# A hybrid decoder block on one Trainium2 core: where the pieces of the MLP's weight sums are made

## The chip, the core and the metric

The kernel runs on one core of a Trainium2 chip. Five engines work side by side, each with its own queue of instructions: TensorE (PE, matmuls), VectorE (DVE), ScalarE (ACT), GpSimd (POOL) and SyncE (SP). In this kernel SP issues most of the DMAs, and POOL and ACT the others. The metric is the time of one execution in device microseconds; less is better.

## What is computed

The block works on S = 2048 tokens of D = 1024 channels in float32. Cut to what matters:

```python
def reference(x, norm_pre_mix, w_in, ..., w_mlp_in, w_mlp_out, norm_post_mlp):
    h = _rmsnorm(x, norm_pre_mix)
    proj = einsum('bsd,de->bse', h, w_in)            # q, k, v, u, z, two gates
    y_attn = _mixer_dilated_attention(q, k, v)       # windows 128, 512, 2048 at dilations 1, 4, 16
    y_gmlp = _mixer_chunked_gmlp(u, z, ...)          # chunks of 128 tokens
    merged = gate_a * (y_attn @ w_branch_attn) + gate_b * (y_gmlp @ w_branch_gmlp)
    x = x + _rmsnorm(merged @ w_out, norm_post_mix)
    h = _rmsnorm(x, norm_pre_mlp)
    a = relu(h @ w_mlp_in)                           # 1024 -> 4096
    y = (a * a) @ w_mlp_out                          # 4096 -> 1024
    return x + _rmsnorm(y, norm_post_mlp)
```

## The kernel before

**Products.** Every float32 operand is split into a high and a low part, and a product is three matmuls (high x high, low x high, high x low). The two large products of the MLP go further: they are cut into quadrants, twice over, and each level needs seven products of sums and differences of quadrants instead of eight. So the first MLP product, w_mlp_in, has an outer level of seven **phases** (o = 0 to 6) and in each phase eight **stages** (two 128-column tiles of the hidden layer each; stages are counted through, so stage 8 is the first of phase o = 1). A stage is seven **products** of six matmuls (L1549). The text counts products through from 0, 56 to a phase, and calls the phases first to seventh.

**What a stage needs.** Its weights come by `load_ha` as the tile `hraw` and are made into half-sums `hs` by `combine` (L1387 to L1402, on POOL, ACT and DVE in turn). The load of a stage takes the buffer of the stage two before it, so it waits until that one's last half-sum, L1402, is done. The activations' quadrants come as `hb` and are split into `spot` tiles. Products land in PSUM tiles `ha`, `hb`, `hc`; DVE (L1563, L1565) and ACT (L1561) add them into the outputs `X`. In the second, fourth and fifth phase a quadrant is first gathered in a stage tile `e` (L1563 makes it, L1565 adds to it). These e tiles live in a pool `rx` under two tags, "xs" and "c1", four buffers each.

**Outer sums.** In the first phase eight `outer_load` / `outer_sum` / `outer_store` steps build sums of the activations' quadrants: three loads `ot`, one sum on DVE (L1504), one on POOL (L1506), one store to `tqd` (L1509). Their tiles use the same two tags of `rx`. The second phase reads `tqd` back as `hb`.

**Pieces of weight sums.** In the third to the sixth phase the weights are no quadrants of w_mlp_in but sums S1 to S4 of them. They are the same for all tokens, and are made ahead in 16 pieces (t = 0 to 15), each four sums of a 128 x 512 tile, stored in DRAM (`wsd`), and loaded from there by `load_ha`. There are two ways to make one:
- In part 2 of the kernel (`merge` and `out_block` for the four chunks of 512 tokens, in the order 2, 3, 0, 1). A generator `w_piece` runs in two calls of `next_piece`: the first issues two loads of 512 KB (`trw`, `tqw`) on SP; the second does four sums on DVE (L1311, L1312, L1314, L1315) and two stores of 512 KB from POOL's queue (L1313, L1316). `trw` and `tqw` have one buffer each. `W_EARLY` pieces are made so, with two `t_piece` of the same kind for the activations between them. `PIECE_AT` says at which of the eight tiles of each chunk's merge a call stands; every out block of the first three chunks has one more, and of the last chunk only the first.
- In the MLP. `w_load` (four loads of 256 KB to `wt`, L1518), four `w_sum` (DVE L1523, POOL L1525, DVE L1527, POOL L1529) and `w_store` (four stores of 256 KB, L1535), all DMAs on SP. Their tiles again use the tags "c1" and "xs" of `rx`, by turns. A table `todo` says after which product each step is written.

**Out block.** For each 128 tokens it multiplies by w_out, adds the result into x (`xr`, L1261), normalizes to `y1` (L1266), transposes y1 on PE (`pt`, L1271), and stores it. The last chunk's out blocks (1,0) to (1,3) lie beside the opening of the MLP.

**What sets the order.** PE's order is written out by hand. The other engines run what the program issues for them in the order of its schedule, and in the MLP as it is written. Each waits at its first instruction that isn't ready; so does SP with its DMAs.

```python
for n in range(8):
    t = 4 + 5 * n
    for f, d, args in ((outer_load, 0, ()), (outer_sum, 4, (0,)), (outer_sum, 6, (2,)), (outer_store, 9, ())):
        later(t + d, f, n, *args)
```

Of the kernel before, what the change touches and what calls it, by code (L numbers as in the profile page):

```python
# [20 lines left out]
KT = 8  # L21
# [21 lines left out]
def block_kernel(ctx, tc, a, out):  # L43
# [1110 lines left out]
    def load_y(c, engs=(("act", "dve"),)):  # L1154
        cs = slice(c * 512, (c + 1) * 512)
        yt = [bot.tile([P, 2, 512], F32R, name=f"yt{c}{k}", tag=f"yt{k}") for k in range(6)]
        for k in range(6):
            split_in(yt[k], ya_d[k, :, cs] if k < 2 else yg_d[k - 2, :, cs], None, *engs[k % len(engs)])
        return yt
# [143 lines left out]
    def w_piece(t):  # L1303

        w, v = (ttp.tile([P, 2, 512], F32, name=f"{n}w{t}", tag=n, bufs=1) for n in ("tq", "tr"))
        for z, n in ((v, t + NF // 2), (w, t)):
            sp.dma_start(z.rearrange("p a c -> p (a c)"), a["w_mlp_in"][n].rearrange("p k c -> p (k c)"))
        yield
        a11, a12, a21, a22 = w[:, 0], w[:, 1], v[:, 0], v[:, 1]
        q, f = divmod(t, 2)  # L1310
        dve.tensor_add(a22, a21, a22)  # L1311
        dve.tensor_sub(a21, a11, a21)  # L1312
        pool.dma_start(ws_d[q][:, 2:4, f], v)  # L1313
        dve.tensor_sub(a11, a22, a11)  # L1314
        dve.tensor_sub(a12, a12, a11)  # L1315
        pool.dma_start(ws_d[q][:, 0:2, f], w)  # L1316
        yield

    W_EARLY = 13
    pieces = deque([w_piece(t) for t in range(W_EARLY - 2)] + [t_piece(0), t_piece(1)] +  # L1320
                   [w_piece(t) for t in range(W_EARLY - 2, W_EARLY)])
    piece = []
    PIECE_AT = {2: (5, 7), 3: (1, 3, 5, 7), 0: (1, 3, 5, 7), 1: (0, 1, 2, 3, 4, 6, 7)}

    def next_piece():
        with behind():
            if piece:
                next(piece.pop(), None)
            elif pieces:
                piece.append(pieces.popleft())  # L1330
                next(piece[0])

    def merge_pieces(c, dt):
        if dt in PIECE_AT[c]:
            next_piece()
# [11 lines left out]
    NQ, HQ = NF // 2, NF // 4  # L1347
# [166 lines left out]
    def w_load(t):  # L1514

        outer_t["w", t] = [rx.tile([P, 512], F32, name=f"wt{t}{m}", tag="xs" if (t - W_EARLY) % 2 else "c1", bufs=4) for m in range(4)]
        for m, z in enumerate(outer_t["w", t]):
# [131 lines left out]
    for n, c in enumerate(chunks):  # L1649
        if n:  # L1650
            mg = merge(c, yt, {0: flush, 2: flush}, lambda dt: merge_pieces(c, dt))
        for i in range(4):
            b = out_block(c, i, mg, flush_older)
            next(b)
            last.append(b)
            if n < 3 or not i:
                next_piece()
            if n < 3 and not i:
                yt = load_y(chunks[n + 1])
                for dt, wch in ((0, 0), (0, 1), (1, 0), (1, 1), (2, 0), (2, 1), (3, 0), (4, 0)):  # L1660
                    with behind():
                        load_gate(chunks[n + 1], dt, wch)
            if n == 3 and i == 1:
                e2r.close()
                egx.close()
                rx = stack(e3, "rx", 1, side="right")
                r4 = stack(e3, "r4", 1, side="right")
                for m in range(4):
                    w = r4.tile([P, 2, 512], F32R, name=f"spot{m}", tag=f"spot{m}")
                    spots.append((w[:, 0], w[:, 1]))  # L1670
                for m in range(2):
                    w = [gtp.tile([P, 512], F32R, name=f"spot{4 + m}{h}", tag=f"gt{m}", bufs=3 - m) for h in range(2)]
                    spots.append(w)
                fifth = gtp.tile([P, 2, 256], F32, name="fifth", tag="gt0", bufs=3)
                first_op(0)
                load_ha(0)
                first_op(1)
                load_ha(1)
                first_op(2)
                for g in sum_ha(0):  # L1680
                    pass
                for j in range(2):
                    for kk in range(2):
                        first_split(j, kk)
                for g in sum_ha(1):
                    pass
                for kk in range(2):
                    first_split(2, kk)
# [225 lines left out]
                       (7, first_split, (6, 0)), (8, first_split, (6, 1)), (9, flush, ())):  # L1914
        later(k, f, *args)
    for n in range(8):
        t = 4 + 5 * n
        for f, d, args in ((outer_load, 0, ()), (outer_sum, 4, (0,)), (outer_sum, 6, (2,)), (outer_store, 9, ())):
            later(t + d, f, n, *args)
    for n in range(NF // 2 - W_EARLY):  # L1920
        t = 7 * 2 * HQ + 6 + 6 * n
        for f, d, args in ((w_load, 0, ()), (w_sum, 4, (0,)), (w_sum, 5, (1,)), (w_sum, 6, (2,)), (w_sum, 7, (3,)),
                           (w_store, 9, ())):
            later(t + d, f, W_EARLY + n, *args)
    for q in range(HQ):
        t = 7 * (5 * HQ + 4) + 19 * q // 2
# [131 lines left out]
```

## Time and profile before

| | |
|---|---|
| time, median of 3 runs | 2632.99 us (2631.65 to 2633.84) |
| the profiled execution | 2633.62 us |
| its span, first to last instruction | 2631.9 us |
| mean granted clock of PE | 0.992 |
| busy: ACT, POOL | 1095.0 us (42%), 1364.3 us (52%) |
| part 2's last out blocks and the first phase | to 1490.5 us |
| second, third, fourth phase | 1490.5 to 1567.5, to 1657.3, to 1734.5 us |

The time of the profiled execution is longer than its span by what lies around it. The rows of the trace below have, in a timeline: start, duration, engine, line, operation, the tiles written and read, the shape, and in brackets the idle time of the engine just before with what ended it. In a list of waits: who waited, for whom, the total in us, how often, the longest. In a group of one tile's instructions: least, median and longest duration in ns, and the first and last start in us. A window's row ends with PE's granted clock, the DMA engines' busy share and GB/s.

### The profile page before, as it was taken

The numbers are of one execution on the slowest core, as the hardware profiler recorded it, in microseconds if no ns is written. First come the engines' busy times: TensorE is split into PE (matmuls) and PEld (weight loads), VectorE is DVE, ScalarE is ACT, GpSimd is POOL, SyncE is SP. The second block draws the span as 40 slices with busy tenths as digits, with TensorE's granted clock in tenths as the row PEclk, the third lists the DMA queues.
The fourth block names the chain that finished last, engine by engine and source line by source line (L and its number), as shares of the span: only waits on it lengthen the run. The fifth ranks groups of instructions, "written<-read, shape, count | busy, mean of one in ns | idle before, by whom it ended". The sixth has DMA issues, their size and how long they took to land. (4 is left out here: it accounts for less than half of the span.)

```text
span 2631.9 us, 35699 instructions
## 1 busy us (share of the span) xinstructions
PE 2561.3 (97%) x12122; PEld 2127.4 (81%) x12122; DVE 1854.8 (70%) x3187; ACT 1095.0 (42%) x2316; POOL 1364.3 (52%) x1265
## 2 busy tenths in 40 slices
PE   9999999999999999999998998999999999999998
PEld 8888888888888887788776886877777888888886
DVE  5676675434433456866667999899898888788867
ACT  5213111254455444544435532433225555555555
POOL 0363354365455554311114656767798677677634
PEclk9999999999999999999999999999999999999999
DMA  8779778888898889776777466456875221222235
GB/s 322 285 245 327 257 234 283 299 276 264 284 303 234 234 293 350 260 246 241 251 236 278 164 179 216 138 183 184 255 248 168 89 88 50 87 94 83 89 119 209
DMA packets 412136, 568.69 MB, mean 216 GB/s; under 512 B 58801, under 2 KB 247473, under 8 KB 410930
## 3 DMA queue, kind: packets, MB, share of 16 engines
q1 hardware_dynamic: 385872, 502.63, 58.4%
q0 software_dynamic: 16192, 57.16, 5.6%
q10 hardware_dynamic: 9890, 6.62, 0.8%
q8 instruction: 96, 1.57, 0.2%
q14 instruction: 86, 0.70, 0.1%
HBM read 362.16 MB, written 204.14 MB: 215 GB/s over the span
## 5 line engine op out<-in xcount | busy, mean ns | idle before, releaser
L1549 PE MATMUL ha<-spot,hs 128*128 128x512 f32 x1344 | 336.3, 397 | 31.1 <-DVE X_yt L1565 9.5
L1549 PEld LDWEIGHTS ha<-spot,hs 128*128 128x128 f32 x1344 | 253.4, 190 | 95.5 <-DVE e L1563 9.9
L1857 PE MATMUL ya<-spot,s 128*128 128x512 f32 x1344 | 323.6, 389 | 2.4 <-DVE X_yt L1865 2.4
L1857 PEld LDWEIGHTS ya<-spot,s 128*128 128x128 f32 x1344 | 252.1, 188 | 55.5 <-issue 1.8
L1549 PE MATMUL hc<-spot,hs 128*128 128x512 f32 x672 | 174.0, 395 | 3.1 <-DVE e L1565 1.7
L728 PE MATMUL g<-opA,spots 128*128 128x512 f32 x672 | 171.4, 399 | 2.1 <-DVE cv L760 2.1
L1857 PE MATMUL yc<-spot,s 128*128 128x512 f32 x672 | 170.5, 389 | 0.0
L728 PE MATMUL g<-opB,spots 128*128 128x512 f32 x648 | 164.0, 397 | 0.0
L1549 PEld LDWEIGHTS hc<-spot,hs 128*128 128x128 f32 x672 | 127.6, 191 | 33.4 <-DVE e L1565 3.4
L96 PE MATMUL x<-hT_a,wq 128*128 128x512 f32 x384 | 149.7, 390 | 0.0
L97 PE MATMUL x<-hT_a,wq 128*128 128x512 f32 x384 | 149.4, 389 | 0.0
L98 PE MATMUL x<-hT_a,wq 128*128 128x512 f32 x384 | 149.4, 389 | 0.0
L1857 PEld LDWEIGHTS yc<-spot,s 128*128 128x128 f32 x672 | 126.1, 188 | 26.2
L728 PEld LDWEIGHTS g<-opA,spots 128*128 128x128 f32 x672 | 121.6, 189 | 24.3 <-issue 2.5
L79 POOL TENSOR_TENSOR spots<-gr,spots 128x512 fp32r<-128x512 f32 x98 | 128.7, 1317 | 21.8 <-DMA gr<-in_w_in_dram 7.7
L79 POOL TENSOR_TENSOR spot<-w2r,spot 128x512 fp32r<-128x512 f32 x79 | 112.1, 1442 | 45.3 <-ACT spot L71 45.3
L1721 ACT ACTIVATE sraw<-sraw 128x1024 f32<-128x1024 f32 x128 | 134.7, 1052 | 2.0 <-DMA sraw<-sd 0.3
L728 PEld LDWEIGHTS g<-opB,spots 128*128 128x128 f32 x648 | 116.9, 188 | 21.2
L71 ACT ACTIVATE hl<-r 128x512 fp32r<-128x512 f32 x48 | 30.4, 633 | 236.5 <-POOL r L329 89.0
L978 DVE TENSOR_REDUCE o<-po 128x256 f32<-128x512 f32 x48 | 33.2, 692 | 134.0 <-PE po L977 134.0
L73 POOL TENSOR_SCALAR spots<-gr 128x512 fp32r<-128x512 f32 x86 | 54.4, 633 | 131.5 <-PE g L728 93.8
L73 POOL TENSOR_SCALAR wq<-wq_r 128x1024 fp32r<-128x1024 f32 x24 | 32.6, 1362 | 136.8 <-PE va L98 87.5
(460 smaller groups left out, 6851.6 us busy)
## 6 DMA issues: line engine op xcount, KB each, us to landing
sraw<-sd SPq DMA_DIRECT2D x128, 256.0 KB, 3.3
qk<-hl SPq DMA_DIRECT2D x24, 1024.0 KB, 5.6
qq<-qk SPq DMA_DIRECT2D x96, 256.0 KB, 5.1
sd<-e SPq DMA_DIRECT2D x64, 256.0 KB, 4.9
hraw<-wsd SPq DMA_DIRECT2D x32, 512.0 KB, 4.6
w2r<-in_w_mlp_out_dram SPq DMA_DIRECT2D x16, 1024.0 KB, 8.7
g<-gated SPq DMA_DIRECT2D x56, 256.0 KB, 5.1
gr<-sgd SPq DMA_DIRECT2D x53, 256.0 KB, 5.0
```

The costliest lines, as they stand in the source:

```text
L71: act.activation(hi, src, AF.Copy)
L73: pool.tensor_scalar(hi, src, 1.0, 1.0, op0=OP.mult, op1=OP.mult)
L79: (pool if lo_eng == "pool" else dve).tensor_sub(lo, src, f32(hi))
L96: pe.matmul(ps, lh, rh, start=start, stop=False)
L97: pe.matmul(ps, lh, rl, start=False, stop=False)
L98: pe.matmul(ps, ll, rh, start=False, stop=stop)
L728: pe.matmul(p, w[:, l, k], h[:, r, k], start=i in (1, 6, 5, 4) and not k and not m, stop=k == 3 and m == 2, skip_group_check=True)
L978: dve.tensor_reduce(ot[:, :, j * 64:(j + 1) * 64], po.rearrange("p (b h e) -> p b e h", b=4, h=2), axis=AX.X, op=OP.add)
L1549: pe.matmul(p, w[:, l, S_AT[i], kk * P:(kk + 1) * P], b[r], start=i in (1, 2, 5) and not kk and not z, stop=kk == 1 and z == 2, skip_group ...
L1721: act.activation(sraw_[n], sraw_[n], func)
L1857: pe.matmul(p, s[:, l], w[r], start=i in (1, 2, 5) and not m and not o, stop=m == 1 and o == 2, skip_group_check=True)
```

## The change

```diff
--- before.py
+++ after.py
@@ -1316,11 +1316,11 @@
         pool.dma_start(ws_d[q][:, 0:2, f], w)
         yield
 
-    W_EARLY = 13
+    W_EARLY = 14
     pieces = deque([w_piece(t) for t in range(W_EARLY - 2)] + [t_piece(0), t_piece(1)] +
                    [w_piece(t) for t in range(W_EARLY - 2, W_EARLY)])
     piece = []
-    PIECE_AT = {2: (5, 7), 3: (1, 3, 5, 7), 0: (1, 3, 5, 7), 1: (0, 1, 2, 3, 4, 6, 7)}
+    PIECE_AT = {2: (3, 5, 7), 3: (0, 2, 4, 6, 7), 0: (1, 3, 5, 7), 1: range(KT)}
 
     def next_piece():
         with behind():
@@ -1653,7 +1653,7 @@
             b = out_block(c, i, mg, flush_older)
             next(b)
             last.append(b)
-            if n < 3 or not i:
+            if n < 3:
                 next_piece()
             if n < 3 and not i:
                 yt = load_y(chunks[n + 1])
@@ -1914,11 +1914,11 @@
                        (7, first_split, (6, 0)), (8, first_split, (6, 1)), (9, flush, ())):
         later(k, f, *args)
     for n in range(8):
-        t = 4 + 5 * n
+        t = 4 + 4 * n
         for f, d, args in ((outer_load, 0, ()), (outer_sum, 4, (0,)), (outer_sum, 6, (2,)), (outer_store, 9, ())):
             later(t + d, f, n, *args)
     for n in range(NF // 2 - W_EARLY):
-        t = 7 * 2 * HQ + 6 + 6 * n
+        t = 38 + 5 * n
         for f, d, args in ((w_load, 0, ()), (w_sum, 4, (0,)), (w_sum, 5, (1,)), (w_sum, 6, (2,)), (w_sum, 7, (3,)),
                            (w_store, 9, ())):
             later(t + d, f, W_EARLY + n, *args)
```

W_EARLY rises from 13 to 14, so 14 pieces are made in part 2 and two in the MLP instead of three. The places of `next_piece` change: merge(2) has tiles 3, 5, 7 instead of 5, 7; merge(3) has 0, 2, 4, 6, 7 instead of 1, 3, 5, 7; merge(1) has all eight instead of seven; out block (1,0) has none any more. That is 32 places for 16 pieces (with the two t_pieces) instead of 30 for 15. The eight outer sums begin at products 4, 8, 12 ... 32 instead of 4, 9, 14 ... 39. The two pieces of the MLP begin at products 38 and 43, in the first phase; the three of before began at 118, 124 and 130, in the third. PE's order is the same.

**The last piece in part 2, on DVE.** Before, behind L1261 of out block (1,0) (which makes xr_10) and the first of its small norm steps. y1_11 is the next out block's tile, r_pm, v_pm and t_pm the norm of y1_10, o_11 a PSUM tile:

```order
L1257 TENSOR_TENSOR y1_11_12726<-o_110_12675,gpost_10420 128x512
L106 RECIPROCAL r_pm10_12656<-r_pm10_12656 128x1
L109 SCALAR_TENSOR_TENSOR t_pm10_12661<-r_pm10_12656,v_pm10_12658 128x1
L113 TENSOR_SCALAR t_pm10_12661<-t_pm10_12661 128x1
L114 TENSOR_TENSOR r_pm10_12656<-r_pm10_12656,t_pm10_12661 128x1
L1266 SCALAR_TENSOR_TENSOR y1_10_12634<-xr_10_12580,r_pm10_12656,gmlp_10421 128x1024
L1311 TENSOR_TENSOR trw12_12577<-trw12_12577 128x512
L1312 TENSOR_TENSOR trw12_12577<-tqw12_12576,trw12_12577 128x512
L1314 TENSOR_TENSOR tqw12_12576<-trw12_12577,tqw12_12576 128x512
L1257 TENSOR_TENSOR y1_11_12726<-o_111_12676,gpost_10420 128x512
L1315 TENSOR_TENSOR tqw12_12576<-tqw12_12576 128x512
```

Now, from that L1261 on:

```order
L1261 SCALAR_TENSOR_TENSOR xr_10_12596<-y1_10_12650,r_post10_12659,xr_10_12596 128x1024
L1311 TENSOR_TENSOR trw13_12562<-trw13_12562 128x512
L105 TENSOR_SCALAR v_pm10_12674<-s2_10_12669 128x1
L1312 TENSOR_TENSOR trw13_12562<-tqw13_12561,trw13_12562 128x512
L1257 TENSOR_TENSOR y1_11_12736<-o_110_12685,gpost_10424 128x512
L1314 TENSOR_TENSOR tqw13_12561<-trw13_12562,tqw13_12561 128x512
L106 RECIPROCAL r_pm10_12672<-r_pm10_12672 128x1
L1315 TENSOR_TENSOR tqw13_12561<-tqw13_12561 128x512
L109 SCALAR_TENSOR_TENSOR t_pm10_12677<-r_pm10_12672,v_pm10_12674 128x1
L113 TENSOR_SCALAR t_pm10_12677<-t_pm10_12677 128x1
L114 TENSOR_TENSOR r_pm10_12672<-r_pm10_12672,t_pm10_12677 128x1
L1266 SCALAR_TENSOR_TENSOR y1_10_12650<-xr_10_12596,r_pm10_12672,gmlp_10425 128x1024
```

The four sums, of piece 13 now instead of 12, stood behind L1266, which makes y1_10, and stand ahead of it.

**The border of the first and second phase, on SP.** Before, from the store of outer sum 6 (ot62) on; hraw_9 and hraw_10 are the weights of stages 9 and 10, hb_20 the activations of the second phase's operand:

```order
L1509 DMA tqd_82<-ot62_13517 128x512
L1378 DMA hraw_9_13621<-in_w_mlp_in_dram 128x2x512
L1509 DMA tqd_82<-ot72_13572 128x512
L1378 DMA hraw_10_13700<-in_w_mlp_in_dram 128x2x512
L1441 DMA hb_20_13773<-tqd_82 128x1024
```

Now, from hraw_9 on. Ahead of it stand the store of ot62, the four loads of piece 14, the store of ot72 and the four loads of piece 15:

```order
L1378 DMA hraw_9_13651<-in_w_mlp_in_dram 128x2x512
L1535 DMA wsd_83<-wt140_13579 128x512
L1535 DMA wsd_83<-wt141_13580 128x512
L1535 DMA wsd_83<-wt142_13581 128x512
L1535 DMA wsd_83<-wt143_13582 128x512
L1378 DMA hraw_10_13738<-in_w_mlp_in_dram 128x2x512
L1535 DMA wsd_83<-wt150_13643 128x512
L1535 DMA wsd_83<-wt151_13644 128x512
L1535 DMA wsd_83<-wt152_13645 128x512
L1535 DMA wsd_83<-wt153_13646 128x512
L1441 DMA hb_20_13815<-tqd_82 128x1024
```

The stores of piece 14 stand ahead of hraw_10, those of piece 15 behind it and ahead of hb_20. e800, the second phase's first stage tile, takes the buffer of wt150.

**The same place on DVE.** Before, the half-sums of stage 8, from L1391 to L1402:

```order
L1391 TENSOR_TENSOR hs_8_13641<-hraw_8_13540,hs_8_13641 128x768
L1565 TENSOR_TENSOR X_xr0_13048<-X_xr0_13048,hc_6_13655 128x512
L1955 TENSOR_TENSOR spot0_12767<-hb_11_13241,spot0_12767 128x512
L1565 TENSOR_TENSOR X_y10_13049<-X_y10_13049,hb_7_13666 128x512
L1398 TENSOR_TENSOR hs_8_13641<-fifth_12775,hs_8_13641 128x256
L1399 TENSOR_TENSOR hs_8_13641<-hraw_8_13540,hs_8_13641 128x256
L1471 TENSOR_TENSOR hb_10_13154<-hb_10_13154 128x512
L1402 TENSOR_TENSOR hs_8_13641<-hraw_8_13540,hs_8_13641 128x512
```

Now:

```order
L1391 TENSOR_TENSOR hs_8_13672<-hraw_8_13560,hs_8_13672 128x768
L1565 TENSOR_TENSOR X_xr0_13058<-X_xr0_13058,hc_6_13686 128x512
L1523 TENSOR_TENSOR wt153_13646<-wt152_13645,wt153_13646 128x512
L1955 TENSOR_TENSOR spot0_12777<-hb_11_13251,spot0_12777 128x512
L1565 TENSOR_TENSOR X_y10_13059<-X_y10_13059,hb_7_13702 128x512
L1398 TENSOR_TENSOR hs_8_13672<-fifth_12785,hs_8_13672 128x256
L1399 TENSOR_TENSOR hs_8_13672<-hraw_8_13560,hs_8_13672 128x256
L1471 TENSOR_TENSOR hb_10_13164<-hb_10_13164 128x512
L1527 TENSOR_TENSOR wt150_13643<-wt153_13646,wt150_13643 128x512
L1402 TENSOR_TENSOR hs_8_13672<-hraw_8_13560,hs_8_13672 128x512
```

Two sums of piece 15 came in between; those of piece 14 stand in the same way around L1402 of stage 7. Between this L1402 and e800 (L1563) stand five instructions, the same as before.

## The prediction

> **What bounds the kernel now.** I read the busy table of the page first.
>
> ```profile
> PE 2561.3 (97%) x12122; PEld 2127.4 (81%) x12122; DVE 1854.8 (70%) x3187; ACT 1095.0 (42%) x2316; POOL 1364.3 (52%) x1265
> ```
>
> TensorE (PE) works 97% of the span, so a change that leaves its matmuls alone can act only on its waits, and on the clock behind a wait. Then I cut the MLP at its phases (56 products of six matmuls each; stretches in us, then length, and per engine the busy time with its instructions).
>
> ```profile
> core 0: us, PE busy (x) PEld busy (x) DVE busy (x) ACT busy (x) POOL busy (x), PEclk, DMA share, GB/s
> 1432.00:1490.50 58.50, 58.23 (x262) 47.99 (x260) 47.42 (x60) 31.50 (x61) 41.86 (x40) 1.00 0.64 221
> 1490.50:1567.50 77.00, 76.41 (x337) 62.94 (x336) 70.31 (x99) 25.76 (x49) 35.59 (x40) 1.00 0.57 171
> 1567.50:1657.30 89.80, 80.55 (x338) 63.27 (x337) 83.69 (x109) 25.16 (x46) 60.47 (x55) 0.98 0.55 182
> 1657.30:1734.50 77.20, 75.21 (x327) 60.66 (x326) 71.98 (x82) 36.22 (x68) 60.61 (x51) 1.00 0.50 162
> ...
> ```
>
> The last part of the first phase has no wait worth a name. The third phase, where the change takes work away, is 12.7 us longer than its neighbours: 89.80 against 77.00 and 77.20. The timeline of PE bounds the stretch in which the waits lie:
>
> ```profile
> 1599.55 1.52 PE L1549 MATMUL ha<-spot,hs 128*128 128x512 f32 x6
> ...
> 1628.43 2.93 PE L1549 MATMUL ha<-spot,hs 128*128 128x512 f32 x6 [3.72 <-DVE X L1565]
> ...
> 1632.80 0.40 PE L1549 MATMUL hb<-spot,hs 128*128 128x512 f32 x1
> ```
>
> Seventeen products begin between 1599.55 and 1632.80, 33.25 us. At the second phase's 77.00 / 56 = 1.375 us they would take 23.4. **So 9.9 us are lost here.** The waits for this phase say on whom:
>
> ```profile
> PE ha L1549 <- DVE X L1565: 5.0, 3, 3.7
> DVE wt L1523 <- DMA wt<-in_w_mlp_in_dram: 1.9, 1, 1.9
> DVE hb L1449 <- DMA hb<-h2d: 1.6, 1, 1.6
> ```
>
> PE waits for VectorE's (DVE) additions into X, and DVE itself twice for a DMA.
>
> **Third phase: what is removed.** Three pieces: twelve loads, six sums on DVE, six on GpSimd (POOL), twelve stores.
>
> ```profile
> L1523 DVE TENSOR_TENSOR wt<-wt,wt x3: 680/681/693, 1594.5 to 1615.3; 128x512 f32<-128x512 f32 x3
> L1525 POOL TENSOR_TENSOR wt<-wt,wt x3: 1284/1289/1295, 1595.3 to 1616.1; 128x512 f32<-128x512 f32 x3
> L1527 DVE TENSOR_TENSOR wt<-wt,wt x3: 909/1159/1206, 1597.9 to 1618.4; 128x512 f32<-128x512 f32 x3
> L1529 POOL TENSOR_TENSOR wt<-wt,wt x3: 1287/1530/1532, 1599.4 to 1621.6; 128x512 f32<-128x512 f32 x3
> DMA to landing us min/median/max: 2.8/5.2/7.0
> ```
>
> DVE loses 3 x 0.68 + 3 x 1.09 = 5.3 us of work, and the 1.9 us that it sat waiting for a piece's data with the X additions queued behind. That is 7.2 us. The 1.6 us for hb also goes if SP, which issues in order, no longer holds hb's loads behind piece stores that wait for POOL: 8.8 us. The measured loss contains a slow clock too:
>
> ```profile
> 1628.40:1632.80 4.40, 4.37 (x12) 0.62 0.34 103
> 1897.40:1901.00 3.60, 3.56 (x9) 0.58 0.19 34
> ```
> ```profile
> PE ha L1549 <- DVE X_gpost L1565: 2.0, 1, 2.0
> ```
>
> After the 3.72 us wait the granted clock is 0.62 and the product takes 2.93 us instead of 1.52: 1.4 us more, which goes with the wait. With 8.8 us less ahead of it DVE would be just in time. What is late next is the same X additions, where DVE is still dense: up to about 2 us of short waits. I take **-9 us**, between -10 (all of the 9.9) and -6.5 (hb still late, and 2 us of short waits).
>
> The second row shows the same price at 1897.4, behind the only wait for X_gpost, which was 2.0 us long (the list of PE's waits). [...]
>
> **Border of phases one and two: what is added.** Pieces 14 and 15 now load at products 38 and 43, add at 42 to 50 and store at 47 and 52. The eight outer sums are drawn together from every fifth to every fourth product to free their buffers. What stands at the border before:
>
> ```profile
> 1471.56 1.77 DVE L1402 TENSOR_TENSOR hs<-hraw,hs 128x512 fp32r<-128x512 f32 x1
> ...
> 1479.89 1.77 DVE L1402 TENSOR_TENSOR hs<-hraw,hs 128x512 fp32r<-128x512 f32 x1
> ...
> 1484.38 1.16 DVE L1391 TENSOR_TENSOR hs<-hraw,hs 128x768 fp32r<-128x768 f32 x1 [0.92 <-ACT hs L1389]
> ...
> 1490.18 1.22 DVE L1402 TENSOR_TENSOR hs<-hraw,hs 128x512 fp32r<-128x512 f32 x1
> ...
> 1494.89 0.67 DVE L1563 TENSOR_TENSOR e<-X_yt,ha 128x512 f32<-128x512 f32 x1
> ```
> ```profile
> 1495.89 1.30 PE L1549 MATMUL ha<-spot,hs 128*128 128x512 f32 x5
> ```
> ```profile
> L1509 SPq DMA_DIRECT2D tqd<-ot x3: 320/320/413, 1473.8 to 1484.1; - x3
> ...
> DMA to landing us min/median/max: 2.0/2.0/4.1
> ```
>
> PE at 1495.89 needs the first tile e800 of phase two. It ends at 1495.56, so there is only about 0.3 us to spare. Between the first of these rows and e800 DVE gets four sums more (2 x 0.68 + 2 x 1.09 = 3.5) and one outer sum less (0.7), and can fill its 0.9 of idle: +1.9. The first sum of piece 14 also waits. It stands directly ahead of the L1402 that now begins at 1479.89. Its fourth tile reuses a buffer of outer 6, whose store to tqd (the first of the three in the last rows, issued 1473.8) lands by 1478; the load behind it takes 2.8 to 5.2 (least and median of the wt row above): 1480.8 to 1483.2. So DVE waits 0.9 to 3.3, and e800 comes at 1494.89 + 2.8 to 5.2 = 1497.7 to 1500.1 by DVE's order alone.
>
> A second wait stands on it: e800 takes the buffer of piece 15's first tile and needs its store landed. SP issues that store behind hraw_10, which waits for the L1402 of stage 8. That one ends now at 1491.4, then at 1494.2 to 1496.6. With 0.9 for the issues and 2.0 (tqd's median, in this quiet stretch) to 5.2 to land, e800 comes at 1497.7 to 1502.7. On POOL the half-sum of stage 8 stands behind piece 14's last sum, some 3 us later than now; I count nothing for it, since DVE, which takes it up, is itself that late. Queued behind e800 on DVE are the half-sums of stage 9 and the next additions; PE waits for the same e800, so they are late together. PE would stand between 2.5 and 7.5 us. I take a value near the lower end, since the nearest rows of landings are the 2.0 and the 2.8: 3.2 us, and 1.3 for the clock behind it. **+4.5 us**, from 0 (SP runs ahead and DVE's operations shorten) to +9 (7.5 and the clock).
>
> **Opening of the MLP: what moves.** In part 2 the last piece's sums move from the second tile of out block (1,0), behind y1, to right behind xr, ahead of y1:
>
> ```profile
> 1378.08 1.28 DVE L1261 SCALAR_TENSOR_TENSOR xr<-y,r_post,xr 128x1024 f32<-128x1024 f32 x1
> ...
> 1382.62 1.28 DVE L1266 SCALAR_TENSOR_TENSOR y<-xr,r_pm,gmlp 128x1024 f32<-128x1024 f32 x1
> 1383.82 0.69 DVE L1311 TENSOR_TENSOR trw<-trw 128x512 f32<-128x512 f32 x1
> ...
> 1386.48 0.68 DVE L1315 TENSOR_TENSOR tqw<-tqw 128x512 f32<-128x512 f32 x1
> ```
>
> ```profile
> L1307 SPq DMA_DIRECT2D tqw<-in_w_mlp_in_dram x1: 328/328/328, 1379.4 to 1379.4; - x1
> ...
> DMA to landing us min/median/max: 3.3/4.1/5.6
> ```
> ```profile
> 1386.65 1.03 PE L1271 MATMUL pt<-ident,y 128*128 128x128 f32 x8
> ```
>
> If piece 13's second half lands as piece 12's does now (issued 1379.4, 4.1 to land), at 1383.5, then three sums of 0.69, the addition of y1's next tile and L1266 follow, and y1 is ready about 1388 instead of 1383.9. Its transposes, now at 1386.65, wait some 1.6 us. This meets two waits that stand there already:
>
> ```profile
> 1410.01 2.92 PE L1549 MATMUL ha<-spot,hs 128*128 128x512 f32 x6 [3.73 <-ACT junk L1256]
> ...
> 1416.55 1.84 PE L1271 MATMUL pt<-ident,y 128*128 128x128 f32 x8 [3.62 <-DVE y L1266]
> ```
>
> They wait for the chain of y1 and of the first half-sums, not for PE: PE arriving 1.6 late shortens them. On the other side the last store leaves about 1.5 us earlier, and with it the first hraw loads; but ACT and POOL now do hraw_1's parts ahead of the tail of the out block. Worked through both orders, y1 of tile 2 comes within 0.4 us of now, and one later load costs about 1. **+1 us**, from -1.5 (the earlier hraw takes part of the 7.35 of waits) to +3 (1.6 and one more product at the slow clock).
>
> **Part 2.** One piece more is 4 x 0.68 = 2.7 us of DVE, 1 MB in and 1 MB out, in merge and out blocks of chunks 2 and 3, whose places shift by one tile. There DVE is far from full:
>
> ```profile
> 1015.00:1110.00 95.00, 89.79 (x412) 73.52 (x411) 65.59 (x111) 40.38 (x68) 26.76 (x25) 0.96 0.86 305
> ```
>
> 65.59 of 95.00. A sum ahead of a gate can lengthen a wait by 0.7, or a moved one shorten it; loads share DMA queues that are 0.86 busy. I take **0**, bounds -2 and +2. The DMA bytes are the same in all, only moved.
>
> **Sum.** -9 + 4.5 + 1 + 0 = -3.5 us. The profiled execution took 2633.62 us (its span 2631.9 and 1.7 around it), 0.63 over the median of the runs shown, 2632.99. So 2630.1 against its own time and, against the median, **2629.5 us**.
>
> **Rivals.**
> - *The border wait does not form.* For it: DVE has 11 us of idle in the 58.50 us before the border, POOL 17; if SP runs ahead, the tile is free before e800. Against: the 0.3 us of room. Then -9 + 0 + 1 = -8, and up to -11 with the opening's gain: about 2625 (2622 to 2627.5). Faster.
> - *Slower: the pieces' landings decide the border.* With 7.0 us, the longest of the wt row, piece 14's last tile is there at 1485 and piece 15's (behind the next tqd store) near 1490. The half-sums of stage 8 then end near 1497, and piece 15's store lands near 1505. PE stands 9.8 us, 11.2 with the clock. With -6.5 in the third phase, where hb's loads would then be late too, and +1 in the opening that is +5.7: about 2638.7. It decides where load and store both land above some 6 us; against it stands that the queues are about as full there (DMA share 0.64 before and 0.57 behind the border) as in the third phase (0.55), where 5.2 was the median.
> - *The third phase's waits are not the pieces'.* X additions and half-sums alone would keep DVE full. For it: the fifth phase is long without a piece, by the same windows:
>
> ```profile
> 1735.00:1824.00 89.00, 83.11 (x351) 66.05 (x350) 81.64 (x111) 31.71 (x58) 57.32 (x53) 0.98 0.63 194
> ```
>
>   Against: the second and the fourth phase, 77 us. If hb's lateness (1.6), the wait behind it and the clock stay, -3 is left: -3 + 4.5 + 1 = +2.5, about 2635.5.
> - *The change does less than it says*: pieces are as many as before, so a mere exchange of one full stretch for another gives 0 +- 2; it lies inside the forecast's case.
>
> **How the numbers follow.** Forecast 0.48 (2627 to 2634), border free 0.30, slower by landings 0.09, third phase not the pieces' 0.13. The measurement tells about 0.2% (5.3 us) from no change. Faster by more, below 2627.7: nearly all of the second case and a little of the forecast's, 0.34. Slower by more, above 2638.3: 0.10. Within: 0.56. The range, 2623 to 2638, leaves out 2 in 10 at most: the deeper part of the free border and most of the slow case.
>
> **What would show it.** Third phase: the wait for X L1565 at 3.7 us is gone and 17 products take some 24 us. Border: a wait of PE on e L1563 near 1499, with L1535 landing or DVE's order as its releaser. Opening: pt waits near 1387, while the two waits near 1410 and 1416 become shorter or one. Wrong would be: a third phase still near 89 us, a border with no wait, or new waits of over 2 us in part 2.

## The result and the profile after

| | before | after |
|---|---|---|
| median | 2632.32 us of 4 runs (2629.9 to 2633.84) | 2648.1 us of 4 runs (2644.21 to 2650.51) |
| ratio, 95% interval | | 1.0052 (1.0037 to 1.0068) |
| the profiled execution, its span | 2633.62, 2631.9 us | 2650.51, 2648.8 us |

The change makes the kernel slower by 0.37 to 0.68%. The profiled execution is the slowest of the four, so what follows, in its own numbers, is some 1 us more than the difference of the medians.

The busy table of the page after (the prediction has the one before):

```profile
PE 2566.1 (97%) x12122; PEld 2128.0 (80%) x12122; DVE 1858.6 (70%) x3189; ACT 1105.1 (42%) x2322; POOL 1367.6 (52%) x1265
```

PE executes the same 12122 matmuls in the same order in both kernels. So the same matmul can be looked up in both traces, and the difference of its start times is how late the changed kernel is at this place. The difference between two such places is what a stage lost:

| place (number of the matmul) | before, us | after, us | late by | lost since the row above |
|---|---|---|---|---|
| end of merge(2) (5700) | 1107.0 | 1107.5 | 0.5 | |
| out block, chunk 3 begins (6080) | 1194.1 | 1199.1 | 5.0 | 4.5 |
| merge(0), middle (6440) | 1274.0 | 1288.2 | 14.2 | 9.2 |
| out block (1,0) begins (6900) | 1379.8 | 1393.4 | 13.6 | -0.6 |
| first phase, product 50 (7340) | 1489.1 | 1505.8 | 16.7 | 3.1 |
| past the border (7690) | 1570.1 | 1594.4 | 24.3 | 7.6 |
| past the third phase's stretch (8000) | 1653.2 | 1667.8 | 14.6 | -9.7 |
| end (12121) | 2621.6 | 2638.2 | 16.6 | 2.0 |

So **part 2 lost 13.1 us**, the opening 3.1, the border 7.6; the third phase gave 9.7 back. The list of PE's waits after, the whole program:

```profile
PE ha L1549 <- DVE e L1563: 11.2, 5, 4.3
PE ha L1549 <- DVE X_yt L1565: 10.1, 8, 3.4
PE pt L1271 <- DVE y L1266: 8.5, 4, 3.5
PE b L96 <- DVE g L1208: 5.7, 5, 3.4
PE ha L1549 <- ACT X_yt L1561: 3.4, 2, 3.2
PE pt L1271 <- ACT tt L1272: 3.1, 1, 3.1
PE o L96 <- ACT mg L71: 2.8, 1, 2.8
```

The wait for X L1565 of the third phase (5.0 before) is not among them any more. New or longer are the ones for y (3.6 before), for g (4.5), for tt and for mg, all of part 2 and the opening.

**Third phase.** Its window is 80.00 us long instead of 89.80, with 103 instead of 109 instructions on DVE:

```profile
1591.80:1671.80 80.00, 77.33 (x337) 62.60 (x336) 75.43 (x103) 25.65 (x46) 52.41 (x49) 1.00 0.41 125
```

The seventeen products of the stretch that took 33.25 us, in the timeline of PE:

```profile
1623.82 1.07 PE L1549 MATMUL ha<-spot,hs 128*128 128x512 f32 x4
...
1646.97 1.30 PE L1549 MATMUL hb<-spot,hs 128*128 128x512 f32 x5
```

They take 23.15 us: all of the loss is gone.

**Border.** The timelines of PE, DVE and ACT there:

```profile
1510.66 1.65 PE L1549 MATMUL ha<-spot,hs 128*128 128x512 f32 x6 [1.97 <-ACT X_y L1561]
1519.36 3.10 PE L1549 MATMUL ha<-spot,hs 128*128 128x512 f32 x8 [4.33 <-DVE e L1563]
```
```profile
1499.15 0.69 DVE L1523 TENSOR_TENSOR wt<-wt,wt 128x512 f32<-128x512 f32 x1 [2.06 <-DMA wt<-in_w_mlp_in_dram]
...
1511.17 1.77 DVE L1527 TENSOR_TENSOR wt<-wt,wt 128x512 f32<-128x512 f32 x1 [1.16 <-POOL wt L1525]
...
1518.63 0.67 DVE L1563 TENSOR_TENSOR e<-X_yt,ha 128x512 f32<-128x512 f32 x1
```
```profile
1506.54 0.42 ACT L1395 ACTIVATE hs<-fifth 128x256 fp32r<-128x256 f32 x1 [5.00 <-POOL fifth L1387]
```

DVE stands 2.06 us at piece 14's first sum for its load, as forecast, and 1.16 at piece 15's second sum for POOL; then e800 begins at 1518.63, behind other work of DVE and without a wait of its own, and PE has waited 4.33 for it. The other wait, 1.97, was not foreseen: ACT stands 5.00 us at a half-sum of stage 8 that POOL makes late, behind the last sum of piece 14, and the copy X_y (L1561) that PE waits for is queued behind it.

**Part 2.** Four waits carry most of the 13 us. In PE's timeline:

```profile
1116.25 0.50 PE L96 MATMUL o<-wo,mg 128*128 128x512 f32 x1 [2.85 <-ACT mg L71]
...
1228.65 1.06 PE L1271 MATMUL pt<-ident,y 128*128 128x128 f32 x8 [3.55 <-DVE y L1266]
...
1279.16 0.80 PE L96 MATMUL b<-yt,wb 128*128 128x512 f32 x1 [3.41 <-DVE g L1208]
```

(the fourth, 0.97 at 1261.1, is again for y). Matmul by matmul they, with the slow clock behind the first and the last (0.64 and 0.50 in the 4 us after), make up the loss: PE falls behind by some 4.2 us at 1116, 3.6 at 1228, 1.2 at 1261 and 4.5 at 1279.

The wait at 1116 does not go back to a load that came late. PE needs mg, which ACT copies (from gates). ACT also makes two halves of w_out (wo) as their loads woraw land. Its rows, before and then after:

```profile
1110.52 1.06 ACT L71 ACTIVATE wo<-woraw 128x1024 fp32r<-128x1024 f32 x1 [2.67 <-DMA woraw<-in_w_out_dram]
1111.48 0.61 ACT L71 ACTIVATE mg<-gates 128x512 fp32r<-128x512 f32 x1
1113.55 1.06 ACT L71 ACTIVATE wo<-woraw 128x1024 fp32r<-128x1024 f32 x1 [1.45 <-DMA woraw<-in_w_out_dram]
```
```profile
1114.11 1.06 ACT L71 ACTIVATE wo<-woraw 128x1024 fp32r<-128x1024 f32 x1 [2.81 <-DMA woraw<-in_w_out_dram]
...
1115.59 0.61 ACT L71 ACTIVATE mg<-gates 128x512 fp32r<-128x512 f32 x1
```

The second half of w_out comes as early as before (1114.11 against 1113.55, with the program 0.5 late), but the copy for PE now stands behind it. So the edit changed not only where the pieces stand: the program's schedule also gave ACT another order. In the groups of ACT's instructions over the whole program this shows as six more loads of its function table, 1.28 us each, before and then after:

```profile
L103 ACT ACT_TABLE_LOAD x8 | 10.3, 1283 | 0.1
L1191 ACT ACT_TABLE_LOAD x4 | 5.1, 1283 | 0.1
```
```profile
L103 ACT ACT_TABLE_LOAD x11 | 14.1, 1283 | 0.2
L1191 ACT ACT_TABLE_LOAD x7 | 9.0, 1283 | 0.1
```

The further six (at 1131.56, 1135.67, 1137.28, 1139.83, 1220.82 and 1224.76) come where a sigmoid of a gate (L1191) now stands between steps of an out block's norm (L103). Neither the prediction nor the experiments below reckoned with this.

The wait at 1228 goes back to gate loads that came late and to one of these table loads. ACT stands for a gate, and the norm's chain behind it starts late; then a table load stands directly ahead of r_pm, for which y waits. Before, none stood there.

```profile
1215.88 0.63 ACT L1191 ACTIVATE g<-g 128x512 f32<-128x512 f32 x1 [2.27 <-DMA g<-gated]
...
1224.76 1.28 ACT L103 ACT_TABLE_LOAD   x1
1226.06 0.29 ACT L103 ACTIVATE r_pm<-s,edge 128x1 f32<-128x1 f32 x1
```

The wait at 1279 is for a gate's load again: ACT stood 3.75 us for one at 1275.31. PE's wait at this place was 1.38 before. In part 2 (1015 to 1400) ACT's waits for the gates' loads sum up to, before and after:

```profile
ACT g L1191 <- DMA g<-gated: 45.1, 27, 5.4
```
```profile
ACT g L1191 <- DMA g<-gated: 56.9, 29, 5.6
```

DVE waited at the pieces' sums for the pieces' own loads, after, 8.0 + 5.8 us (before 5.2):

```profile
DVE trw L1311 <- DMA trw<-in_w_mlp_in_dram: 8.0, 2, 5.7
DVE trw L1312 <- DMA tqw<-in_w_mlp_in_dram: 5.8, 2, 3.8
```

But 2.32 and 3.84 of these lie behind 1393 and belong to the opening; in part 2 itself DVE stood 7.6 against 5.2.

Why the gates' loads come late can in part be read from SP's timeline, ahead of the wait at 1228.65 (SP issues in order):

```profile
1197.65 0.33 SPq L1307 DMA_DIRECT2D trw<-in_w_mlp_in_dram  x1
1198.08 1.05 SPq L92 DMA_DIRECT2D yt<-yad  x2
1201.20 0.33 SPq L1307 DMA_DIRECT2D tqw<-in_w_mlp_in_dram  x1
1201.62 1.81 SPq L92 DMA_DIRECT2D yt<-ygd  x4
1203.52 6.01 SPq L1182 DMA_DIRECT2D g<-gated  x7
```

tqw has one buffer. The store of the piece before (issued by POOL at 1197.05) landed 4.1 us later, at 1201.14; SP stood until then, and four of the loads of yt and those of the gates g came after it. The same place before:

```profile
1192.44 0.33 SPq L1307 DMA_DIRECT2D tqw<-in_w_mlp_in_dram  x1
...
1195.71 7.48 SPq L1182 DMA_DIRECT2D g<-gated  x8
```

There SP stood for the store as well, and longer (from 1187.4). What changed is when: PE begins chunk 3's out block at 1194.1 before and at 1199.1 after, so the gates' loads begin 1.6 us behind it before and 4.4 after, and the eighth of them, which before went out with the others, comes only behind the next piece's trw, at 1216.90. They also take longer to land, in the median 5.1 us before (from 1195 to 1215) and 7.8 after (from 1200 to 1220):

```profile
g<-gated SPq DMA_DIRECT2D x8, 256.0 KB, 5.1
```
```profile
g<-gated SPq DMA_DIRECT2D x8, 256.0 KB, 7.8
```

merge(2) and merge(3) each have one place more, so loads and sums are exchanged only between the two; from chunk 3's out blocks to the middle of merge(1) they stand at the tiles of before, one piece further on. Yet 9.2 of the 13.1 us are lost there.

### The profile page after: what moved, and what is told of

Same layout as the page of the kernel before. It is cut to its first block, busy times and chain, and to the rows that moved or that the text cites. A ratio compares the mean times of both kernels' runs of the same rounds, so it can differ in the third digit from the quotient of the medians.

```text
span 2648.8 us, 35701 instructions
## 1 busy us (share of the span) xinstructions
PE 2566.1 (97%) x12122; PEld 2128.0 (80%) x12122; DVE 1858.6 (70%) x3189; ACT 1105.1 (42%) x2322; POOL 1367.6 (52%) x1265
## 5 line engine op out<-in xcount | busy, mean ns | idle before, releaser
L96 PE MATMUL o<-wo,mg 128*128 128x512 f32 x256 | 103.1, 403 | 2.9 <-ACT mg L71 2.8
```

Source lines behind the costliest of these rows:

```text
L96: pe.matmul(ps, lh, rh, start=start, stop=False)
```

## The experiments

For each kernel the same comparison of matmul starts gives the loss by stage. The columns are those of the table above: part 2 from matmul 5700 to 6900, opening to 7340, border to 7690, third phase to 8000, the rest. The numbers are single profiled executions. Kernels whose part 2 is that of the kernel before (e2, h1, g1, v4) read -1.3 to +3.9 there, and the rest reads -0.8 to +4.0 throughout, so differences below some 4 us in these two columns say little. The border's column is steadier: -0.1 to 0.3 without a piece in the first phase, 7.1 to 8.3 with two. The profiled executions of f1, f2 and f5 were the shortest of theirs, some 4 to 5 us below their medians, so their losses may read too low by as much.

| kernel | ratio to before, 95% | part 2 | opening | border | third | rest |
|---|---|---|---|---|---|---|
| the change | 1.0052 (1.0037 to 1.0068) | 13.1 | 3.1 | 7.6 | -9.7 | 2.0 |
| e1_part2_only | 1.0049 (1.0031 to 1.0067) | 13.7 | 2.3 | -0.1 | -1.2 | -0.8 |
| e2_mlp_only | 1.0007 (0.9996 to 1.0018) | 3.9 | -0.7 | 7.8 | -8.4 | 1.6 |
| e3_first_places | 1.0047 (1.0031 to 1.0063) | 16.1 | -3.7 | -0.1 | -1.7 | 2.9 |
| e4_late_places | 1.0010 (0.9994 to 1.0025) | -0.9 | 6.1 | -0.1 | -2.2 | 2.0 |
| e5_loads_on_pool | 1.0049 (1.0031 to 1.0067) | 7.0 | 5.2 | 8.2 | -9.7 | 1.8 |
| f1_no_piece_loads | 0.9981 (0.9967 to 0.9995) | -3.6 | -3.6 | 7.8 | -9.8 | 1.5 |
| f2_no_piece_sums | 1.0023 (1.0008 to 1.0037) | 7.7 | -5.1 | 8.3 | -9.8 | 2.6 |
| f4_no_piece_stores | 0.9974 (0.9963 to 0.9985) | -6.5 | 1.4 | 7.1 | -9.8 | 1.2 |
| f5_no_sums_loads_on_pool | 1.0032 (1.0020 to 1.0044) | 6.3 | 1.6 | 7.1 | -9.8 | 2.0 |
| h1_one_in_first | 0.9999 (0.9989 to 1.0008) | -0.9 | -0.2 | 3.7 | -3.9 | 4.0 |
| g1_last_sum_behind | 0.9999 (0.9987 to 1.0012) | 0.7 | 0.3 | 5.0 | -5.7 | 0.7 |
| e6_before_loads_on_pool | 1.0008 (0.9997 to 1.0019) | 3.2 | 1.1 | 0.3 | -1.5 | 2.7 |
| v4_later_sums | 1.0004 (0.9994 to 1.0014) | -1.3 | -0.9 | -0.1 | 2.0 | 1.9 |
| e8_late_places_on_pool | 1.0022 (1.0013 to 1.0032) | 3.0 | 4.4 | -0.1 | -3.3 | 0.6 |

**Part 2 alone** (the change, with the MLP's two tables as before):

```diff
-        t = 4 + 4 * n
+        t = 4 + 5 * n
-        t = 38 + 5 * n
+        t = 7 * 2 * HQ + 6 + 6 * n
```

> Part 2 as in the change (14 pieces, the new places), the MLP as before: outer sums every fifth product, and the two pieces that are left at products 118 and 124 of the third phase. Theory (the places in part 2 are the loss): PE is about 13 us late at the end of merge(1) and 16 after the opening; the border has no new wait; the third phase gains some 3 us of its 9.9, since one of three pieces is gone: about 2645 us. Rival (the loss in part 2 belongs to the whole program's order, not to the places): within 3 us of the kernel before, 2632.

Measured: 2644.81 us. Part 2 loses as in the change, the border nothing. The loss belongs to the places in part 2 and to what follows from them. The third phase gains 1.2 with two pieces in place of three, less than the 3 expected.

**The MLP's side alone** (the kernel before, with):

```diff
-        t = 4 + 5 * n
+        t = 4 + 4 * n
-        t = 7 * 2 * HQ + 6 + 6 * n
+        t = 38 + 5 * n if n < 2 else 7 * 2 * HQ + 6 + 6 * n
```

> Part 2 as before (13 pieces, old places), the MLP's side of the change: outer sums every fourth product, pieces 13 and 14 at products 38 and 43; piece 15 stays in the third phase, at product 118. Theory: no difference in part 2, the border costs about 7.6 us as in the change (DVE's first stage tile e800 waits for a piece's store), the third phase gains 6 to 8: about 2632 (2630 to 2635). Rival (the border's cost comes from part 2's late data or its late opening): border under 3 us, 2627.

Measured: 2633.9 us. The border costs 7.8 without the change's part 2, so it isn't the late opening's. The two waits are there again, 2.15 for X_y and 4.33 for e. What two pieces cost in the first phase is what they cost in the third.

**The first and the last place alone, 13 pieces** (the kernel before, with):

```diff
-    PIECE_AT = {2: (5, 7), 3: (1, 3, 5, 7), ...
+    PIECE_AT = {2: (3, 5, 7), 3: (1, 3, 5, 7), ...
-            if n < 3 or not i:
+            if n < 3:
```

> 13 pieces, and of the change's places only the first (merge(2) at tiles 3, 5, 7) and the last (none in out block (1,0)); merge(3) and merge(1) as before, so that loads and sums change places in all of merge(3), 0 and 1. MLP as before. Theory (what costs is a piece's load that stands on SP ahead of gate loads, and a load that waits on the landing of the stores of a piece next to it): the first wait near 1113 (PE on ACT mg, +4) is there, and, since places stay two tiles apart, merge(3) and its out blocks lose under 2: about 2637. Rival (each further piece's DVE sums cost): no loss, 2632.

Measured: 2643.86 us. There is no further piece here, yet part 2 loses 16.1. The wait near 1113 is there (3.44 on ACT mg), though not for a load ahead of the gates as my theory had it, but by ACT's order, as in the change. It missed the rest: I expected under 2 where places stay two tiles apart. Loads and sums have changed places throughout, ACT has eight table loads more than before, and PE's wait for the evacuated gates and ACT's wait for their loads have grown, in part 2 (before: 4.5 and 45.1):

```profile
PE b L96 <- DVE g L1208: 10.6, 4, 5.1
```
```profile
ACT g L1191 <- DMA g<-gated: 61.4, 30, 5.2
```

So it isn't the number of pieces that costs, but which tile each half of a piece falls into, with the order on ACT that comes of it.

**The further piece at the end instead** (the kernel before, with):

```diff
-    W_EARLY = 13
+    W_EARLY = 14
-    ... 1: (0, 1, 2, 3, 4, 6, 7)}
+    ... 1: range(KT)}
-            if n < 3 or not i:
+            if n < 3 or i < 2:
```

> 14 pieces with the places of before up to merge(1) tile 4, and two further places, merge(1) tile 5 and out block (1,1), so that the four places of tiles 4 to 7 and the two of the last out blocks hold two pieces. MLP as before, two pieces in its third phase. Theory (the loss of part 2 comes from where loads and stores fall among the gate and w_out loads of chunks 2, 3 and 0): no loss up to product 1 of merge(1), then 2 to 6 us from the last pieces in the opening, third phase 3 less: 2632 to 2636. Rival (the further piece costs wherever it stands): 2640 or more.

Measured: 2634.95 us. With the old places part 2 loses nothing, and ACT has no further table load there, though its waits for the gates' loads sum up to 54.1 us, nearly as in the change. Up to matmul 6900 there are as many pieces as before; the further one lies in the opening and costs 6.1 there, where PE waits 5.4 for the first half-sums:

```profile
PE ha L1549 <- ACT hs L1389: 5.4, 2, 4.3
```

**Loads on another queue** (the change, with `pool.dma_start` for `sp.dma_start` in `w_piece`; SP no longer stands at a piece's load):

> The change, with the loads of the pieces in part 2 issued from GpSimd's queue, where their stores are, instead of SyncE's. Theory (SP stands in front of a piece's load until the store before has landed, and the yt and gate loads behind it come late): SP no longer stands, most of the 13 us of part 2 come back, at least 7, about 2638. Rival (DMA bandwidth or the DVE sums are what costs): the bytes and sums are the same, so 2645 to 2650 as the change.

Measured: 2644.7 us, all but the rival's time, although part 2 loses 7.0 instead of 13.1. Two more us were lost in the opening, and PE waits 2.9 us on ACT mg near 1120, for another tile than in the change, with no load of a piece ahead of a gate on SP. The edit did more than free SP: the six table loads more are gone as well, so the difference of 6 isn't SP's alone.

**Leaving out parts of the pieces.** Without the loads of twelve of the fourteen w pieces (the same tiles are summed and stored again and again), and without the sums:

```diff
...
-        for z, n in ((v, t + NF // 2), (w, t)):
+        for z, n in ((v, t + NF // 2), (w, t)) if t in (0, W_EARLY - 2) else ():
```

> The change, with the loads of the w pieces in part 2 left out but for two of fourteen (the same tiles are summed and stored again; what the later phases read is then not the weight sums). DVE's sums and all stores stay. Theory (the loss in part 2 comes from the loads: DVE stands at a sum until its load has landed, SP stands at a load until the store before has landed, and 1 MB more is in the queues): part 2 up to the end of merge(1) loses under 4 us of its 13, about 2638 or less. Rival (the sums' own time on DVE, 56 x 0.69 us): 2645 to 2650 as the change.

```diff
-        dve.tensor_add(a22, a21, a22)
-        dve.tensor_sub(a21, a11, a21)
...
-        dve.tensor_sub(a11, a22, a11)
-        dve.tensor_sub(a12, a12, a11)
```

> The change, with the four sums of each w piece in part 2 left out: loads and stores stay, each store waits for its load alone (the later phases then read plain weights). Theory as for the kernel without loads, and its finer question: if DVE standing at the sums is the larger part, most of the loss of part 2 goes (loss under 5 at the end of merge(1)); if SP's standing and the full DMA queues are, over 8 us of it stay.

Measured: 2627.78 and 2637.35 us. Without loads part 2 is faster than the kernel before, with the sums of all pieces in it. With e3, which has no further sums and loses 16.1, this says that the sums' own time is not what costs. Without sums, and so with no place at which DVE could stand for a w piece's load, 7.7 of the 13.1 stay.

To part the rest, without sums and with the loads on POOL's queue (neither DVE nor SP stands, the bytes stay), and without the stores of the first twelve w pieces (half of the bytes gone, nothing for the next load to wait on; DVE's sums stay):

```diff
-        for z, n in ...: sp.dma_start(...)
+        for z, n in ...: pool.dma_start(...)
```

> The change without the four sums of the w pieces in part 2 (later phases read plain weights) and with their loads on GpSimd's queue: neither DVE nor SP stands for a piece; its bytes are in the DMA queues as before. From product 5700 (end of merge(2)) to 6900 (last out blocks) the change lost 13 us, without sums 7.7, with loads on GpSimd's queue 7.0. Theory A (bytes in full DMA queues are what is left in both): 5 to 7 lost still. Theory B (the two standings are nearly all, each about half): under 2 lost.

```diff
-        pool.dma_start(ws_d[q][:, 2:4, f], v)
+        if t >= W_EARLY - 2:
+            pool.dma_start(ws_d[q][:, 2:4, f], v)
...
-            src = ws_d[q][:, WS_AT.index(name)]
+            src = ws_d[6][:, WS_AT.index(name)]
```

> The change with the stores of the w pieces in part 2 left out but for the last two of fourteen (later phases read those two's sums throughout). The loads on SP then no longer wait for a store's landing, half of the pieces' bytes is gone, DVE's sums and their waits for loads stay. Theory A (bytes and SP's standing): from product 5700 to 6900 under 4 us lost of 13. Theory B (DVE standing at the sums for the loads): 6 or more.

Measured: 2641.0 and 2624.94 us. With neither engine standing 6.3 us are lost in part 2; without the stores, and with DVE still waiting 8.1 us at its sums, nothing is.

These runs don't part the loss cleanly. The kernel before was not run with the same things left out, except for the loads on POOL's queue: there it reads 3.2 itself (e6_before_loads_on_pool below), so that of the 7.0 with the new places some 4 are the places', not more than the noise. And each edit changes ACT's order again. Against the kernel before, the change and e1 have six table loads more, e3 and f2 eight, f4 four, and all others none. Table loads alone don't decide it, since f4 has four more and loses nothing, and e5 and f5 have none more and lose 7.0 and 6.3. The sum of ACT's waits for the gates' loads doesn't either: 54.1 in e4, which loses nothing, and 56.1 in f5; kernels with the old part 2 read 45.1 (before), 48.7 (v4) and 51.0 (e2). What the runs do show: the moved places cost 13 to 16 us with the loads on SP, and some 4 with them on POOL's queue. How much of it is SP standing, the transfers, or ACT's order stays open.

**One piece in the first phase** (the MLP's side alone, with one piece there and two in the third phase):

```diff
+        t = 38 if not n else 7 * 2 * HQ + 6 + 6 * n
```

> Part 2 as before (13 pieces), outer sums every fourth product, and of the three pieces of the MLP one in the first phase, at product 38, in buffers of tag c1, and two in the third phase, at 124 and 130. So e800, of tag xs, no longer waits for a piece's store, and DVE has two sums more ahead of it instead of four. Theory (the border's 7.8 us are the waits for landings at L1523 and the second piece's store ahead of e800): border under 3 us; third phase gains 3 to 5: about 2630 to 2632. Rival (any piece there costs its share, half of the 7.8): border 4, in all 2633.

Measured: 2632.75 us, and the rival is right: the border costs 3.7, half of 7.8, though e800 waits for no store of a piece. In PE's timeline:

```profile
1493.43 1.66 PE L1549 MATMUL ha<-spot,hs 128*128 128x512 f32 x6 [1.56 <-ACT X_y L1561]
1499.21 3.03 PE L1549 MATMUL ha<-spot,hs 128*128 128x512 f32 x12 [1.38 <-DVE e L1563]
```

Then with that piece's last POOL sum and its stores three products later, behind the half-sum that ACT waits for:

```diff
-            later(t + d, f, W_EARLY + n, *args)
+            later(t + d + (3 if not n and d in (7, 9) else 0), f, W_EARLY + n, *args)
```

> One piece in the first phase as in h1_one_in_first, its last POOL sum L1529 three products later, behind the half-sum of stage 8 on POOL, and its stores too. Theory (POOL stands at L1529 for DVE's L1527, the half-sum L1387 comes late, ACT stands 5 us at L1395 with X_y of L1561 behind it, and PE waits 1.6 for that): this wait is gone and the border costs about 2 instead of 3.7: 2630 to 2631. Rival (PE then waits the same time at the next product, for e800): border 3.7 as before, 2632 to 2633.

Measured: 2633.1 us. The wait on ACT is gone, and PE waits longer for e800:

```profile
1500.62 5.49 PE L1549 MATMUL ha<-spot,hs 128*128 128x512 f32 x12 [2.72 <-DVE e L1563]
```

The border costs 5.0 here, no less than with the wait on ACT. The order on POOL decides at which product PE waits; undoing it gains nothing. What delays e800 is DVE's order: two further sums here, four in the change, with DVE's waits at them.

**Towards a faster version.** The kernel before with the pieces' loads on POOL's queue; with the third phase's sums and stores two products later (sums at +6 to +9, stores at +11); and the late places with the loads on POOL's queue:

> The kernel before with the loads of the pieces in part 2 issued from GpSimd's queue instead of SyncE's. Theory (SP standing at a piece's load costs in the kernel before too, only less, since its places are two tiles apart): 2 to 5 us less, about 2629. Rival (with the old places SP's standing is hidden, and DVE stands longer at the sums because the loads leave later): 2632 to 2636.

> The kernel before, with the sums and stores of the three pieces in the third phase two products later behind their loads (sums at +6 to +9, stores at +11). Theory (of the 9.9 us that the third phase loses, 1.9 are DVE standing at the first sum until its load has landed, and the rest the sums' own work): that wait of 1.9 us goes, third phase 2 us shorter, 2630. Rival (the X additions are dense there anyway and the stores now stand ahead of hb's later loads): no change or 2 us more.

> 14 pieces at the places of before plus two late ones (as in the kernel with late places, 1.001 of before), with the pieces' loads on GpSimd's queue. Theory: SP no longer stands in merge(1) and in the opening; the 5.8 us lost there shrink to 2 or 3, the third phase keeps its 2 to 3 us: 2629 to 2631. Rival: DVE stands for later landings instead, 2635.

Measured: 2636.66, 2633.88 and 2639.11 us. None beats the kernel before; in all three the rival was nearer. In v4 the wait for the piece's load is gone, but POOL waits 5.7 us for a load of hb; what made it late is not shown:

```profile
PE ha L1549 <- DVE X L1565: 6.9, 2, 4.1
...
POOL hb L1449 <- DMA hb<-h2d: 5.7, 1, 5.7
```

## Why the prediction was wrong

- **Third phase, -9.** Right: -9.7 measured, and the reason holds. The waits on X went with the six DVE sums, and the slow clock behind the last one with them (granted 1.00 over the phase, 0.98 before). Of the "up to about 2 us of short waits" none came.
- **Border, +4.5, from 0 to +9.** Right in mechanism, short in size: 7.6, and 7.8 alone. The term that was mis-sized is "3.2 us, and 1.3 for the clock": PE stood 6.3 us (4.33 for e800 and 1.97 for X_y), and 1.3 is left for the clock, granted 0.61 in the 4 us from 1519.3 on. The 3.2 was taken near the lower end by the nearest landings, but landings did not set it. In DVE's order e800 comes 7.0 us later against PE (1518.63 against 1494.89, less the 16.7 by which the program was late already), not 2.8 to 5.2: the wait for piece 14's load was 2.06 and inside its bounds, but the four sums took 4.3 us instead of 3.5, and the wait of 1.16 for POOL was not counted. The second wait, for a store, did not come, and h1_one_in_first, where none can, costs half for half of the sums. The step on POOL, "I count nothing for it, since DVE, which takes it up, is itself that late", had the path wrong, since ACT takes the half-sum up first and has X_y queued behind it; but g1_last_sum_behind shows nothing lost on top, as it said.
- **Opening, +1, from -1.5 to +3.** 3.1 measured, at the top of the range. y of out block (1,0) was late as argued, because DVE waits at the sums for piece 13's loads (2.32 and 3.84 us in DVE's timeline), but its transposes waited 2.92, not 1.6, and a stall of 3.13 for the next block's tt came on top. Behind them the waits of 3.73 and 3.62 shrank to 0 and 1.05, as forecast, and gave part of it back.
- **Part 2, 0, from -2 to +2: this is where the prediction fell**, 13.1 us and outside of every case. The step was "There DVE is far from full ... A sum ahead of a gate can lengthen a wait by 0.7 ...; loads share DMA queues that are 0.86 busy". It priced one further piece by its sums, and took the moved transfers for free because their bytes were only moved. The runs show that the places cost, and not the piece: moved places without a further piece lose 16.1 (e3_first_places), the change's part 2 alone 13.7 (e1_part2_only), and a further piece at the end, with the other places as they were, nothing in part 2 and 6.1 in the opening (e4_late_places). Two things were taken as they had been, without a reason. One is the other loads in these full queues: in the change the gates' loads begin later against PE, land in 7.8 us instead of 5.1 in the stretch shown, and PE's waits at 1228 and 1279 go back to them. The other is the order on ACT: it changed, and the wait at 1116 and the table load ahead of the one at 1228 come of that. The prediction asks only whether DVE is full.
- **The rivals.** "The border wait does not form" was wrong, "the pieces' landings decide the border" named the right place with too long landings, and none of them lay in part 2. The range and the chances were drawn from the MLP almost alone, with 2 us either way for part 2.

What stays open: how the 13 us of part 2 divide between the late loads and ACT's new order, and which single transfer costs which wait. No run moves the places and keeps ACT's order as it was; and part 2 differs by up to 5 us between executions whose program there is the same.

## What to carry to other kernels

In a stretch whose DMA queues are as full as here (0.86), price a moved transfer by the loads that it lands among and by what is queued behind it on the issuing engine, and not by its bytes or by the compute that goes with it. After an edit, compare the order of every engine that the program's schedule sets, also of those that the edit doesn't name: here one copy on ACT behind another half of w_out, and six table loads more, came unasked. A pair of alternating steps (load, sum) that is shifted by one place changes every pair after it until a second shift, so the whole stretch has to be read, not the place of the edit. When work is taken out of a stretch where an in-order engine is full (here DVE, busy for 83.69 of 89.80 us), look first whether the place that it goes to has the room at all: two pieces cost in the first phase what they cost in the third (7.8 and 8.4 us in e2_mlp_only).

## What was not expected of the hardware

In the changed kernel the granted clock behind a wait did not follow from the wait's length. Four windows of 4 us each after a wait of the changed kernel (columns: window, length, PE busy, granted clock, DMA share, GB/s), behind waits of 2.85, 3.55, 3.41 and 1.97 us:

```profile
1116.30:1120.30 4.00, 4.00 (x11) 0.64 0.75 276
1228.60:1232.60 4.00, 3.95 (x22) 1.00 0.41 131
1279.20:1283.20 4.00, 4.00 (x10) 0.50 0.73 227
...
1510.70:1514.70 4.00, 4.00 (x18) 1.00 0.08 4
```

Behind the wait of 3.55 the clock was 1.00 in the mean of its window, behind those of 2.85 and 3.41 it was 0.64 and 0.50. PE's timeline has the same: its 128x512 matmuls begin every 0.43 us from 1117.63 to 1120.19 and from 1279.76 to 1284.03, and every 0.23 us from 1120.95, from 1284.80 and, behind the wait of 3.55, from 1229.78 on. The loss in the table includes this: past 1279 the program fell 4.6 us behind (9.6 to 14.2) where the wait had grown by 2.0 only, from 1.38 to 3.41. Length alone did not decide here, since 2.85 was followed by a slow stretch and 3.55 by none; what did is not shown.
